# Gate and up projections as seven block products in Strassen's form, with sums of weights by adding transfers and VectorE

## The chip, the cores and the metric

The kernel runs on one core of one Trainium2 chip. A core has five engines with their own instruction streams: TensorE (PE), which multiplies matrices and loads its standing operand by separate weight loads (PEld), VectorE (DVE), ScalarE (ACT), GpSimd (POOL) and SyncE (SP), which issues transfers. [...] The metric is the device time of one execution in microseconds, the median of several runs; lower is better.

## The reference

512 tokens of width 1024 go through two layers. Each layer is half a gated FFN, a mixer (a short convolution, or attention over the tokens, each beside an attention over a memory of 256 rows), and half a gated FFN again; so there are four FFNs, each with 2816 hidden features.

```python
D_MODEL = 1024
SEQ = 512
D_FF = ((8 * D_MODEL // 3 + 255) // 256) * 256
...
def swiglu(h, w_gate_up, w_down):
    gu = h @ w_gate_up
    gate, up = gu[..., :D_FF], gu[..., D_FF:]
    return (jax.nn.silu(gate) * up) @ w_down
...
        x = x + 0.5 * swiglu(rmsnorm(x, ffn_norm[l, 0]), ffn_w_gate_up[l, 0], ffn_w_down[l, 0])
...
        x = x + 0.5 * swiglu(rmsnorm(x, ffn_norm[l, 1]), ffn_w_gate_up[l, 1], ffn_w_down[l, 1])
    return rmsnorm(x, final_norm)
```

## The kernel before

**Numbers.** Everything is held with the features on the 128 partitions and the 512 tokens along the free side, so x is eight tiles of 128x512. Values are fp32, and each operand of a product is split into two parts of type float32r, a high part (a copy that rounds) and a low part (the value less the high part). A product over 128 rows is then three matmuls, high by high, high by low and low by high (mm3, L134 to L136), each with a weight load of its own.

**Weights.** The class Weights takes the weights in pieces of 128x1024, that is 8 blocks of 128x128, in the order of use. A piece is loaded by SyncE into one of 4 buffers (wr, L63), three pieces ahead, and split two pieces ahead: the high part by ACT (wh, L81), the low part by DVE (wl, L82), into 3 buffers each. Since the buffers go round, a split waits until TensorE has read the piece that held the buffer before.

**An FFN.** Its 22 hidden tiles of 128 features stand in two halves of 11. For a hidden tile, project is called for the gate and again for up: 8 blocks of rows by mm3, 24 matmuls of 512 columns into one of 7 PSUM banks (mm). Then DVE multiplies the gate by 1 / rms of the tokens (L287), ACT takes Silu (L288), DVE multiplies by up (L289), and ACT and DVE split the hidden tile (L139, L140). The norm's gain is taken into x ahead of the products (Normed, L143), and 1 / rms behind them, so that products begin before the sums of squares (Stats, L155 and L159) are there; the matmuls that spread 1 / rms over the partitions (step1, L162 to L176, in the bank aux) stand after the first 2 of 8 blocks of the first up product. After each half, down takes 8 tiles of x, each by 11 x 3 matmuls of 512 columns; DVE adds them to x (L308, L311), and in the second half the next norm's gain and squares follow tile by tile. In the last FFN the last tile is taken by halves of 256 tokens with the final norm between (Last, L721 to L806).

**The order.** Each engine runs its instructions in the order in which the program gives them after scheduling; an instruction that waits holds what stands behind it on its engine. The core of the FFN is

```python
pg, pu = project(nd), project(nd, mid=st.step1 if begin else None)
...
nc.vector.tensor_tensor(out=t, in0=pg, in1=st.row, op=ALU.mult)
nc.scalar.activation(t, t, AF.Silu)
nc.vector.tensor_tensor(out=t, in0=pu, in1=t, op=ALU.mult)
hid.append(parts())
split(t, *hid[-1])
```

Of the kernel before, what the change touches and what calls it, by code (L numbers as in the profile page):

```python
# [16 lines left out]
P = 128  # L17
T = 512
# [4 lines left out]
HALVES = [(0, 11), (11, 22)]  # L23
# [12 lines left out]
class Weights:  # L36
    """Pieces of the weights in the order of use: loaded ahead, and split ahead into two float32r
    parts."""

    LOAD, SPLIT = 3, 2  # L40

    def __init__(self, nc, pool):
        self.nc, self.pool = nc, pool
        self.todo, self.raw, self.parts = [], {}, {}
        self.loaded = self.split = self.used = 0

    def add(self, ap, widths=(1024, 1024), step=1024):
        at = 0
        for w in widths:
            self.todo.append((ap[:, at : at + w], step))  # L50
            at += w
        assert at == ap.shape[1]

    def load(self):
        """The next piece, by transfers of step columns."""
        n = self.loaded
        self.loaded += 1
        ap, step = self.todo[n]
        w = ap.shape[1]
        self.raw[n] = self.pool.tile([P, 1024], F32, tag="wr", name=f"wr{n}", bufs=4)  # L60
        for a in range(0, w, step):
            c = slice(a, min(a + step, w))
            self.nc.sync.dma_start(out=self.raw[n][:, c], in_=ap[:, c])  # L63
            yield

    def begin(self):
        """The next piece's parts, split by step columns."""
        i = self.split
        self.split += 1
        while self.loaded < min(len(self.todo), i + 1 + self.LOAD):  # L70
            for _ in self.load():
                pass
        ap, step = self.todo[i]
        w, raw = ap.shape[1], self.raw.pop(i)
        hi = self.pool.tile([P, 1024], F32R, tag="wh", name=f"wh{i}", bufs=3)
        lo = self.pool.tile([P, 1024], F32R, tag="wl", name=f"wl{i}", bufs=3)
# [9 lines left out]

    def next(self, ahead=SPLIT):
        """The next piece's parts; the splits run ahead of it by so many pieces."""
        i = self.used
        self.used += 1  # L90
        while self.split < min(len(self.todo), i + 1 + ahead):
            for _ in self.begin():
                pass
        return self.parts.pop(i)
# [3 lines left out]
def model(ctx: ExitStack, tc: tile.TileContext, A, out):  # L98
# [13 lines left out]
    SLOTS = {"s": 66, "t": 12}  # L112
# [7 lines left out]
    def bank(tag="mm", n=T):  # L120
        bufs = {"mm": 7, "aux": 1}[tag]
        return ppool.tile([P, n], F32, tag=tag, name=name(tag), bufs=bufs)
# [5 lines left out]
    selr = cpool.tile([64, NH], F32R, name="selr")  # L128
    ident = cst[:, C_ID : C_ID + P]
    ones = cst[:, C_ONE : C_ONE + P]  # L130

    def mm3(ps, wh, wl, xh, xl, first, last):
        """One product over 128 rows: high x high, high x low, low x high."""
        nc.tensor.matmul(ps, wh, xh, start=first, stop=False)  # L134
        nc.tensor.matmul(ps, wh, xl, start=False, stop=False)  # L135
        nc.tensor.matmul(ps, wl, xh, start=False, stop=last)  # L136
# [10 lines left out]
    class Stats:  # L147
        """The squares of tiles of 128 features, summed; then 1 / rms by token."""
# [13 lines left out]
        def step1(self, c=None):  # L162
            """The sums over all features, on every partition, and their roots."""
# [14 lines left out]
        def columns(self):  # L178
            """1 / rms of the tokens of each block, by partition."""
# [10 lines left out]
    class Normed:  # L190
        """Tiles of x times a norm's gain, in two parts; 1 / rms is applied behind the product."""
# [13 lines left out]

    def plan_ffn(n):
        for a, b in HALVES:
            chunks(A["gu"][n, a:b])
            for d in range(KD):
                W.add(A["dn"][n, d][:, a * P : b * P], (6 * P, 5 * P))  # L210
# [30 lines left out]
    # The tensor engine's clock rises while it works: it does from the first transfers on.  # L241
    zero = slot(dt=F32R)
    nc.vector.memset(zero.bitcast(F32), 0.0)
    warm = bank()
    for _ in range(10):
        nc.tensor.matmul(warm, zero[:, :P], zero, start=True, stop=True)
# [4 lines left out]
    def project(nd, n=T, mid=None):  # L251
        """The next piece of weights, 128 of its columns by all rows, times tiles of tokens."""
# [8 lines left out]
    def project_tokens(nd, nb, mid={}):  # L261
        """Four pieces of weights move, 512 columns; the tokens stand: 128 of them in each bank."""
# [12 lines left out]
    def ffn(n, x, nd, st, cols, fresh=False, last=None):  # L275
        """x + swiglu / 2, and the statistics and gains of the next norms. With last, the final
        norm, which takes the last tile by halves of the tokens."""
        nst, nxt = Stats(), [Normed(c) for c in cols]
        new = list(x)
        for h, (a, b) in enumerate(HALVES):  # L280
            m = b - a
            hid = []
            for j in range(m):
                begin = st.row is None
                pg, pu = project(nd), project(nd, mid=st.step1 if begin else None)
                t = slot("t")
                nc.vector.tensor_tensor(out=t, in0=pg, in1=st.row, op=ALU.mult)  # L287
# [7 lines left out]
            for d in range(KD):  # L295
# [23 lines left out]
                if end:  # L319
                    for q in nxt:  # L320
                        q.add(d, y)
# [580 lines left out]
```

## Time and profile before

| what | value |
|---|---|
| median of 3 runs (lowest, highest) | 2036.88 us (2036.84, 2038.18) |
| span of the profiled execution | 2038.5 us |
| TensorE busy in it | 99% |
| VectorE, ScalarE, GpSimd busy | 49%, 35%, 2% |
| bytes moved | 195.73 MB |

The profile is of one execution, and its span stands beside the median as the time of that execution. Busy times are for each engine apart, in us and as a share of the span. In a timeline a row gives start and length of an instruction, its engine, line and operation, what it writes and reads, its shape, and in brackets how long the engine had stood idle and what ended that. A matmul's length holds its way through the array, which the next one overlaps, so the rate of a stream is read from the distance of the starts.

### The profile page before, as it was taken

To read this page: it belongs to the slowest core of one execution; us is meant where nothing else is said; L and a number is where in the kernel's file an instruction comes from. 1 tells how busy PE (TensorE), PEld (TensorE's weight loads), DVE (VectorE), ACT (ScalarE), POOL (GpSimd) and SP (SyncE) were. 2 spreads that over 40 slices of the span, in tenths; PEclk is the share of its full clock that TensorE was granted. 3 is DMA by queue.
4 is the path that set the end of the run, shared out by engine and by line. 5 is a ranking of instruction groups with operands and counts; after the bars stand their busy time and mean duration, and the time that the engine had idled before them with its cause. 6 is when DMAs were issued, how large, how long until landed. Compare 5 with 4: busy or idle time off the path is not lost.

```text
span 2038.5 us, 22628 instructions
## 1 busy us (share of the span) xinstructions
PE 2018.4 (99%) x9175; PEld 1674.7 (82%) x9175; DVE 1002.9 (49%) x1355; ACT 704.7 (35%) x1049; POOL 34.1 (2%) x50
## 2 busy tenths in 40 slices
PE   9999999999999999999999999999999999999997
PEld 8788888888888888888888888888878878888886
DVE  7643434576555443443644343467546664344444
ACT  7422222353224332232432222335335552222233
POOL 2000000000000000000000000000001100000000
PEclk9999999999999999999999999999999999999998
DMA  7322332332222323322322332232221032233222
GB/s 261 105 94 79 117 99 82 99 104 73 98 99 93 100 84 91 118 94 76 120 94 86 91 114 98 80 112 77 80 93 63 32 103 94 84 102 106 98 78 70
DMA packets 62328, 195.73 MB, mean 96 GB/s; under 512 B 7056, under 2 KB 9232, under 8 KB 62224
## 3 DMA queue, kind: packets, MB, share of 16 engines
q1 hardware_dynamic: 62224, 194.30, 30.0%
q8 instruction: 71, 1.16, 0.2%
q14 instruction: 33, 0.27, 0.0%
HBM read 192.17 MB, written 2.10 MB: 95 GB/s over the span
## 4 chain that ended last, share of the span: by engine, by line
PE 98%; DVE 1%; DMA 0%; issue 0%; ACT 0%; SPq 0%; DVEq 0%; ACTq 0%
PE mm L134 32%; PE mm L135 32%; PE mm L136 32%; PE mm L694 0%; PE mm L434 0%; DVE wl L82 0%; DMA s<-in_memT 0%; PE aux L651 0%; DVE s L143 0%; PE mm L666 0%; PE mm L750 0%; PE aux L134 0%; PE aux L136 0%; PE aux L135 0%; PE mm L785 0%
## 5 line engine op out<-in xcount | busy, mean ns | idle before, releaser
L134 PE MATMUL mm<-s,wh 128*128 128x512 f32 (+1 forms) x2763 | 1067.5, 386 | 2.4 <-ACT s L143 1.5
L135 PE MATMUL mm<-s,wh 128*128 128x512 f32 (+1 forms) x2763 | 1066.6, 386 | 0.3
L136 PE MATMUL mm<-s,wl 128*128 128x512 f32 (+1 forms) x2763 | 1066.0, 386 | 0.5 <-DVE wl L82 0.5
L81 ACT ACTIVATE wh<-wr 128x1024 fp32r<-128x1024 f32 (+3 forms) x403 | 390.4, 970 | 1174.1 <-PE mm L135 749.9
L134 PEld LDWEIGHTS mm<-s,wh 128*128 128x128 f32 x2763 | 519.0, 188 | 108.1 <-ACT s L143 2.4
L136 PEld LDWEIGHTS mm<-s,wl 128*128 128x128 f32 x2763 | 518.9, 188 | 105.9 <-DVE wl L82 1.1
L135 PEld LDWEIGHTS mm<-s,wh 128*128 128x128 f32 x2763 | 519.2, 188 | 104.7 <-DVE s L143 0.7
L82 DVE TENSOR_TENSOR wl<-wr,wh 128x1024 fp32r<-128x1024 f32 (+3 forms) x403 | 449.3, 1116 | 190.9 <-ACT wh L81 189.0
L289 DVE TENSOR_TENSOR t<-mm,t 128x512 f32<-128x512 f32 x88 | 60.9, 692 | 289.9 <-PE mm L136 287.0
L287 DVE TENSOR_TENSOR t<-mm,r 128x512 f32<-128x512 f32 x88 | 60.8, 691 | 224.6 <-PE mm L136 224.5
L308 DVE SCALAR_TENSOR_TENSOR t<-mm,r 128x512 f32<-128x512 f32 (+1 forms) x65 | 44.4, 683 | 124.8 <-PE mm L136 124.8
L140 DVE TENSOR_TENSOR s<-t,s 128x512 fp32r<-128x512 f32 (+1 forms) x128 | 86.4, 677 | 2.2 <-ACT s L139 2.0
L139 ACT ACTIVATE s<-t 128x512 fp32r<-128x512 f32 (+1 forms) x128 | 78.6, 616 | 16.5 <-DVE t L547 6.2
L143 DVE SCALAR_TENSOR_TENSOR s<-s,vec,s 128x512 fp32r<-128x512 f32 (+1 forms) x64 | 49.0, 780 | 14.6 <-ACT s L143 14.6
L288 ACT ACTIVATE t<-t 128x512 f32<-128x512 f32 x88 | 54.2, 616 | 3.1 <-DVE t L287 3.1
L143 ACT ACTIVATE s<-s,vec 128x512 fp32r<-128x512 f32 (+1 forms) x64 | 42.9, 688 | 33.3 <-DVE s L311 32.8
L311 DVE TENSOR_TENSOR s<-s,t 128x512 f32<-128x512 f32 (+1 forms) x65 | 45.2, 696 | 0.6
L352 DVE TENSOR_TENSOR s<-s,mm 128x512 f32<-128x512 f32 x32 | 21.8, 686 | 42.3 <-PE mm L136 42.3
L135 PE MATMUL mm<-wl,s 128*128 128x512 f32 x96 | 38.2, 398 | 4.4 <-DVE wl L82 4.4
L155 ACT ACTIVATE t<-s 128x512 f32<-128x512 f32 x59 | 35.9, 617 | 14.1 <-DVE s L311 14.1
L140 DVE TENSOR_TENSOR s<-mm,s 128x512 fp32r<-128x512 f32 (+1 forms) x56 | 34.2, 646 | 12.2 <-ACT s L139 12.1
L686 POOL TENSOR_TENSOR s<-s,s 128x128 fp32r<-128x128 f32 x32 | 13.9, 466 | 1558.8 <-ACT s L685 1558.8
(116 smaller groups left out, 743.7 us busy)
## 6 DMA issues: line engine op xcount, KB each, us to landing
wr<-in_gu SPq DMA_DIRECT2D x176, 512.0 KB, 3.7
wr<-in_dn SPq DMA_DIRECT2D x64, 384.0 KB, 3.1
wr<-in_dn SPq DMA_DIRECT2D x64, 320.0 KB, 2.9
wr<-in_ain SPq DMA_DIRECT2D x28, 512.0 KB, 3.7
wr<-in_wout SPq DMA_DIRECT2D x24, 512.0 KB, 3.7
wr<-in_mkv SPq DMA_DIRECT2D x14, 512.0 KB, 5.2
wr<-in_wq SPq DMA_DIRECT2D x8, 512.0 KB, 3.7
wr<-in_wv SPq DMA_DIRECT2D x8, 512.0 KB, 3.7
```

Source lines behind the costliest of these rows:

```text
L81: self.nc.scalar.activation(hi[:, c], raw[:, c], AF.Copy),
L82: self.nc.vector.tensor_tensor(out=lo[:, c], in0=raw[:, c], in1=hi[:, c].bitcast(F32), op=ALU.subtract),
L134: nc.tensor.matmul(ps, wh, xh, start=first, stop=False)
L135: nc.tensor.matmul(ps, wh, xl, start=False, stop=False)
L136: nc.tensor.matmul(ps, wl, xh, start=False, stop=last)
L139: nc.scalar.activation(hi, src, AF.Copy)
L140: nc.vector.tensor_tensor(out=lo, in0=src, in1=hi.bitcast(F32), op=ALU.subtract)
L143: return nc.scalar.activation(hi, src, AF.Copy, scale=g), nc.vector.scalar_tensor_tensor(out=lo, in0=src, scalar=g, in1=hi.bitcast(F32), o ...
L287: nc.vector.tensor_tensor(out=t, in0=pg, in1=st.row, op=ALU.mult)
L288: nc.scalar.activation(t, t, AF.Silu)
L289: nc.vector.tensor_tensor(out=t, in0=pu, in1=t, op=ALU.mult)
L311: nc.vector.tensor_tensor(out=y[:, c], in0=new[d][:, c], in1=t[:, c], op=ALU.add)
```

## The change

**What is computed.** Two hidden tiles make a pair. The gate and up weights of one hidden tile (an item) are a matrix of 2 x 2 blocks: gate and up by the first and the second 512 features of x. x is a matrix of 2 x 2 blocks too: first and second 512 features by first and second 256 tokens. Their product is worked out in Strassen's form (Winograd's variant), with seven block products in place of eight: each has 4 blocks of 128 rows, mm3 and 256 columns, so that a pair takes 7 x 2 x 4 x 3 = 168 matmuls of 256 columns, where it took 2 x 2 x 8 x 3 = 96 of 512. UNITS names the seven by their combination of x, in the order of use: B11, B21, T3, T4, T2, T1, B22.

**Weights.** A pair's weights are seven pieces of 128x1024: four blocks and combinations of them. Two of the sums are made by transfers: SyncE loads the first block, and a transfer issued by GpSimd adds the second to it in SBUF (tile ws, 3 buffers; lines 93 and 95). Two are made by DVE in place (L127). Each piece is split by ACT (L118) and DVE (L119) as before, seven for two hidden tiles where it was four. Buffers: wr 5, wh and wl 4, loads 8 ahead.

**x.** Quads and Quad form the seven combinations of x for the next FFN: a scaled copy by ACT, four sums of 256 columns by GpSimd for two tiles of x, and the splits of the results.

**Banks.** The 7 + 1 banks become three doubles (mm, one for an item of the pair) and two aux. Other stages take halves of the doubles.

**Behind the products**, in the class Gated: the products of the item are added up in its two banks, partly by TensorE, which adds to what stands in a bank. ACT copies B11's sum to where B21 is added (L471, the seed) and copies T3 (L475) and T2 (L477) aside; DVE adds T2 to where T4 and T3 stood (L478), adds to T1 (L480), multiplies up by -1 / rms (L482) and gate by 1 / rms (L488); ACT takes Silu (L492); GpSimd multiplies the two by halves of the tokens (L494); the split of the hidden tile is L211 and L212. TensorE starts an item's B21 behind its L471, T4 behind L475, T1 behind L478 and B22 behind L482. The next pair's first items take the double banks in turn.

**Order.** Pairs 0 to 4, down of pairs 0 to 3, pairs 5 to 7, down of 4 to 6, pairs 8 to 10, down of 7 to 10: 8, 6 and 8 hidden tiles in place of 11 and 11. Down products stay plain. step1 is called when the first pair's B11 is finished with its late rows: products of the first two rows of B11 and B21 of both items stand ahead, with a matmul of zeros that starts the third double. Between FFNs the memory's keys and values and one x are written to DRAM and read back (keep), which makes room in SBUF.

```diff
-HALVES = [(0, 11), (11, 22)]
+GROUPS = [(0, 4), (4, 7), (7, 11)]
-    LOAD, SPLIT = 3, 2
+    LOAD, SPLIT = 8, 2
+    PIECE = [0, 1, 3, 2, 0, 4, 1]
+    BUFS = {"wr": 5, "ws": 3, "wh": 4, "wl": 4}
+    def block(self, ap):
+        w = ap.shape[1] // 4
+        item = {"ap": [ap[:, i * w : (i + 1) * w] for i in range(4)], "w": w, "raw": [None] * 5}
+        self.units += [(item, q) for q in range(7)]
...
+        w, (a11, a12, a22, a21) = item["w"], item["ap"]
+        for i, first, more in {
+            0: [(0, a11, None)], 1: [(1, a12, None)], 2: [(3, a11, a21)], 3: [(4, a21, a22), (2, a22, None)]
+        }.get(q, []):
+            t = item["raw"][i] = self.tile("ws" if more is not None else "wr")
+            self.nc.sync.dma_start(out=t[:, :w], in_=first)
+            if more is not None:
+                self.nc.gpsimd.dma_start(out=t[:, :w], in_=more, accum_op=ALU.add)
...
+        for at, to, of in ((3, 0, 4), (5, 1, 0)):
+            if q == at:
+                r = item["raw"]
+                self.nc.vector.tensor_tensor(out=r[to][:, :w], in0=r[to][:, :w], in1=r[of][:, :w], op=ALU.add)
...
+    class Quad:
+        def __init__(self, b1, b2):
+            ts = slot("t"), slot("t")
+            b11, b12, b21, b22 = b1[:, :H], b1[:, H:], b2[:, :H], b2[:, H:]
+            t1, t3, t2, t4 = ts[0][:, :H], ts[0][:, H:], ts[1][:, :H], ts[1][:, H:]
+            tt = nc.gpsimd.tensor_tensor
+            tt(out=t3, in0=b22, in1=b12, op=ALU.subtract)
+            tt(out=t1, in0=b11, in1=b12, op=ALU.subtract)
+            tt(out=t2, in0=t1, in1=b22, op=ALU.add)
+            tt(out=t4, in0=t2, in1=b21, op=ALU.subtract)
+            self.of = {}
+            self.two(b11, "B11")
+            self.four(b2, "B21", "B22")
+            self.four(ts[0], "T1", "T3")
+            self.two(t2, "T2", True)
+            self.two(t4, "T4")
...
+    def order_ffn(pair, down):
+        pair(0)
+        for i, (a, b) in enumerate(GROUPS):
+            for p in range(a + 1, b):
+                pair(p)
+            if i + 1 < len(GROUPS):
+                pair(b)
+            down(i)
...
+    UNITS = ["B11", "B21", "T3", "T4", "T2", "T1", "B22"]
+    def products(items, quads, early=()):
+        nk = len(quads)
+        late = [k for k in range(nk) if k not in early]
+        qs = []
+        for it in items:
+            it.seeded = not early
+            qs.append((banks(), it.seeded))
+        held = []
+        def product(i, u, n, w, ks):
+            q, seeded = qs[i]
+            at = {"B21": 0, "T3": T + H, "T4": T + H}.get(n, T)
+            ps = q[:, at : at + H]
+            for k in ks:
+                c = slice((i * nk + k) * P, (i * nk + k + 1) * P)
+                first = k == (early or late)[0] and (n == "B11" or n == "B21" and not seeded)
+                mm3(ps, w[0][:, c], w[1][:, c], *quads[k].of[n], first, True, True, k == ks[0])
+            return ps
+        for u, n in enumerate(UNITS):
+            w = W.next()
+            for i, it in enumerate(items):
+                if u < 2 and early:
+                    ps = product(i, u, n, w, early)
+                    held.append((i, it, u, n, w))
+                else:
+                    ps = product(i, u, n, w, list(range(nk)))
+                    it(n, ps, qs[i][0])
+            if u == 1 and early:
+                third = nc.tensor.matmul(banks()[:, :H], zero[:, :P], zero[:, :H], start=True, stop=True)
+                tc.keep_in_program_order(third)
+                for i, it, u_, n_, w_ in held:
+                    it(n_, product(i, u_, n_, w_, late), qs[i][0])
...
-                pg, pu = project(nd), project(nd, mid=st.step1 if begin else None)
-                t = slot("t")
-                nc.vector.tensor_tensor(out=t, in0=pg, in1=st.row, op=ALU.mult)
-                nc.scalar.activation(t, t, AF.Silu)
-                nc.vector.tensor_tensor(out=t, in0=pu, in1=t, op=ALU.mult)
-                hid.append(parts())
-                split(t, *hid[-1])
+        class Gated:
+            def __init__(self, j):
+                self.j, self.a, self.b = j, slot("t"), slot("t")
+            def __call__(self, n, ps, q):
+                both = q.rearrange("p (a t) -> p a t", t=T)
+                y, c, z = q[:, :H], q[:, H:T], q[:, T + H :]
+                a, b = self.a, self.b
+                if n == "B11":
+                    if p_first(self.j):
+                        st.step1()
+                        turned()
+                    to = y if self.seeded else b[:, :H]
+                    nc.scalar.activation(to, ps, AF.Copy)
+                elif n == "B21" and not self.seeded:
+                    nc.vector.tensor_tensor(out=y, in0=y, in1=b[:, :H], op=ALU.add)
+                elif n == "T3":
+                    nc.scalar.activation(a[:, :H], ps, AF.Copy)
+                elif n == "T2":
+                    nc.scalar.activation(a[:, H:], ps, AF.Copy)
+                    nc.vector.tensor_tensor(out=z, in0=z, in1=a[:, H:], op=ALU.add)
+                elif n == "T1":
+                    nc.vector.tensor_tensor(out=c, in0=ps, in1=a[:, :H], op=ALU.add)
+                    nc.vector.tensor_tensor(
+                        out=b.rearrange("p (a t) -> p a t", t=H), in0=both[:, :, H:],
+                        in1=less[0].rearrange("p (a t) -> p a t", t=H), op=ALU.mult,
+                    )
+                elif n == "B22":
+                    g = slot("t")
+                    nc.vector.tensor_tensor(
+                        out=g.rearrange("p (a t) -> p a t", t=H), in0=both[:, :, :H],
+                        in1=st.row.rearrange("p (a t) -> p a t", t=H), op=ALU.mult,
+                    )
+                    nc.scalar.activation(g, g, AF.Silu)
+                    for o, i in ((slice(0, H), slice(H, T)), (slice(H, T), slice(0, H))):
+                        nc.gpsimd.tensor_tensor(out=g[:, o], in0=g[:, o], in1=b[:, i], op=ALU.mult)
+                    hid[self.j] = parts()
+                    split(g, *hid[self.j])
...
+        def pair(p):
+            products([Gated(2 * p), Gated(2 * p + 1)], quads, (0, 1) if p == 0 else ())
```

On DVE of the kernel before stand, in the second FFN, for a hidden tile and the start of the next (mm the products of gate and up, r is 1 / rms, t the tile that is worked on, s parts of hidden tiles, wr, wh and wl the pieces of the weights):

```order
L287 TENSOR_TENSOR t_467_4951<-mm_465_4895,r_461_4858 128x512
L82 TENSOR_TENSOR wl137_4923<-wr137_4805,wh137_4922 128x1024
L140 TENSOR_TENSOR s_464_4886<-t_462_4881,s_463_4885 128x512
L289 TENSOR_TENSOR t_467_4951<-mm_466_4926,t_467_4951 128x512
L82 TENSOR_TENSOR wl138_4962<-wr138_4836,wh138_4961 128x1024
L140 TENSOR_TENSOR s_469_4956<-t_467_4951,s_468_4955 128x512
L287 TENSOR_TENSOR t_472_5021<-mm_470_4965,r_461_4858 128x512
L82 TENSOR_TENSOR wl139_4993<-wr139_4889,wh139_4992 128x1024
```

Each product is read by one instruction, and a split of weights stands between two of them.

On DVE of the changed kernel stand, in the third pair of the same FFN, from the T2 products to the scaling of up (mm_547 and mm_548 are the double banks of items 0 and 1, nr is -1 / rms, ws a sum made by transfers):

```order
L119 TENSOR_TENSOR wl532_7006<-wr516_6795,wh531_7005 128x1024
L478 TENSOR_TENSOR mm_547_6843<-mm_547_6843,t_543_6839 128x256
L127 TENSOR_TENSOR wr516_6795<-wr516_6795,ws525_6913 128x1024
L119 TENSOR_TENSOR wl534_7038<-wr519_6849,wh533_7037 128x1024
L478 TENSOR_TENSOR mm_548_6844<-mm_548_6844,t_545_6841 128x256
L480 TENSOR_TENSOR mm_547_6843<-mm_547_6843,t_543_6839 128x256
L127 TENSOR_TENSOR wr519_6849<-wr519_6849,wr516_6795 128x1024
L482 TENSOR_TENSOR t_544_6840<-mm_547_6843,nr_512_6146 128x512
L480 TENSOR_TENSOR mm_548_6844<-mm_548_6844,t_545_6841 128x256
L119 TENSOR_TENSOR wl537_7092<-ws522_6882,wh536_7091 128x1024
L482 TENSOR_TENSOR t_546_6842<-mm_548_6844,nr_512_6146 128x512
```

Between the additions into the banks (L478, L480) and the scaling (L482) of the two items now stand two sums of weights (L127) and two splits (L119), and item 1's L478 stands ahead of item 0's L480.

On ACT of the changed kernel stand, from there on into the next pair (items mm_559 and mm_560):

```order
L477 ACTIVATE t_543_6839<-mm_547_6843 128x256
L118 ACTIVATE wh533_7037<-wr519_6849 128x1024
L477 ACTIVATE t_545_6841<-mm_548_6844 128x256
L118 ACTIVATE wh536_7091<-ws522_6882 128x1024
L492 ACTIVATE t_549_7055<-t_549_7055 128x512
L118 ACTIVATE wh539_7123<-wr526_6916 128x1024
L211 ACTIVATE s_550_7060<-t_549_7055 128x512
L492 ACTIVATE t_552_7076<-t_552_7076 128x512
L471 ACTIVATE mm_559_7089<-mm_559_7089 128x256
L118 ACTIVATE wh542_7154<-wr516_6795 128x1024
L211 ACTIVATE s_553_7081<-t_552_7076 128x512
L471 ACTIVATE mm_560_7090<-mm_560_7090 128x256
```

The split wh533 stands ahead of item 1's copy of T2 (L477), wh536 ahead of the Silu of item 0 (L492), and the seeds of the next pair (L471) behind Silu and split of the hidden tiles of this pair.

244 lines of the change are left out of this document (162 added, 82 removed).

## The prediction

> **What bounds the kernel now.** The page is read first: the busy shares, then the chain that ended last, then the costliest group of TensorE with the idle time ahead of it. Its columns there are busy time, mean ns of one and idle time with its releaser.
>
> ```profile
> span 2038.5 us, 22628 instructions
> PE 2018.4 (99%) x9175; PEld 1674.7 (82%) x9175; DVE 1002.9 (49%) x1355; ACT 704.7 (35%) x1049; POOL 34.1 (2%) x50
> PE 98%; DVE 1%; DMA 0%; issue 0%; ACT 0%; SPq 0%; DVEq 0%; ACTq 0%
> L134 PE MATMUL mm<-s,wh 128*128 128x512 f32 (+1 forms) x2763 | 1067.5, 386 | 2.4 <-ACT s L143 1.5
> ```
>
> TensorE holds 98% of the chain, and its commonest matmul waited 2.4 us in all. So every matmul taken away is worth its spacing, and every wait put into its stream costs its full length. The view of waits says the same: the longest one of TensorE on VectorE (total, times, longest) is
>
> ```profile
> PE mm L135 <- DVE wl L82: 4.4, 2, 3.7
> ```
>
> A stretch of the gate and up products shows the slack of the others (length, then busy time and count of PE, PEld, DVE, ACT, POOL, then granted clock, DMA share, GB/s):
>
> ```profile
> 560.00:600.00 40.00, 40.00 (x178) 33.10 (x177) 21.47 (x27) 10.65 (x12) 0.00 (x0) 1.00 0.31 105
> ```
>
> DVE is busy 54% and ACT 27% of the time there, so neither is a bound by its load; what they can cost is latency.
>
> **The price of a matmul.** The last tile of the last down product runs at 512 columns and then by halves of 256, which gives both spacings in one timeline of TensorE (start, length).
>
> ```profile
> 2004.83 0.39 PE L135 MATMUL mm<-s,wh 128*128 128x512 f32 x1
> ...
> 2015.25 0.39 PE L136 MATMUL mm<-s,wl 128*128 128x512 f32 x1
> 2015.48 0.28 PE L134 MATMUL mm<-s,wh 128*128 128x256 f32 x1
> ...
> 2018.59 0.28 PE L136 MATMUL mm<-s,wl 128*128 128x256 f32 x1
> 2018.71 0.50 PE L750 MATMUL mm<-cst,t 128*128 128x1 f32 x4
> ```
>
> From 2004.83 to 2015.48 there are 47 steps of 0.2266 us; from 2015.48 to 2018.71 there are 27 of 0.1196. I use 0.2267 and 0.120, so half the columns cost 0.53 of the time. Before: 4 FFNs x 22 tiles x 2 x 8 x 3 = 4224 gate and up matmuls, x 0.2267 = 957.6 us. After: 4 x 11 pairs x 168 = 7392 of 256 columns, x 0.120 = 887.0. **The stream gains 70.6 us**, or 21.76 - 20.16 = 1.60 a pair. The down products keep 528 matmuls in each FFN and gain nothing.
>
> The Trainium skill, "TensorE: Matmul & The Clock Gate", section Back-to-back issue gap, speaks against the change: it gives a stream of load and matmul pairs about 131 ns at 512 columns and 81 at 128, on a line between them about 98 at 256 (an estimate). By that a pair would go from 12.6 to 16.4 us and the change would lose some 170 us in TensorE alone. The trace doesn't agree: its stream of such pairs stands at 226.6 ns; the formula for an isolated matmul on the same page, 518 and 262 cycles at 2.4 GHz, lies nearer and would make the gain 104 us.
>
> **What the epilogue costs.** After an item's seven products, its two banks pass back through ACT and DVE between products, and TensorE waits for them at five places. The durations: first a gate tile of before, whose last matmul releases DVE, and ACT's split that releases DVE's.
>
> ```profile
> 99.73 0.39 PE L136 MATMUL mm<-s,wl 128*128 128x512 f32 x1
> 99.98 1.06 ACT L81 ACTIVATE wh<-wr 128x1024 fp32r<-128x1024 f32 x1 [3.83 <-PE mm L135]
> 100.16 0.69 DVE L287 TENSOR_TENSOR t<-mm,r 128x512 f32<-128x512 f32 x1 [2.70 <-PE mm L136]
> 101.08 1.23 DVE L82 TENSOR_TENSOR wl<-wr,wh 128x1024 fp32r<-128x1024 f32 x1 [0.22 <-ACT wh L81]
> ```
>
> The matmul ends at 100.12 and DVE starts at 100.16; ACT ends at 101.04 and DVE starts at 101.08: a hand-over is 0.04 us (I take 0.06 to TensorE). Queued behind one another on DVE they overlap by 0.09:
>
> ```profile
> 43.52 0.41 DVE L504 TENSOR_TENSOR t<-mm,r 128x256 f32<-128x256 f32 x1
> 43.85 1.21 DVE L82 TENSOR_TENSOR wl<-wr,wh 128x1024 fp32r<-128x1024 f32 x1
> ...
> 57.63 1.21 DVE L82 TENSOR_TENSOR wl<-wr,wh 128x1024 fp32r<-128x1024 f32 x1
> 58.76 0.74 DVE L143 SCALAR_TENSOR_TENSOR s<-s,vec,s 128x512 fp32r<-128x512 f32 x1
> ```
>
> that is 0.33 for 256 columns and 1.13 for 1024 until the next one starts, and by the same 0.09 about 0.60 for 512. The smaller forms, by group:
>
> ```profile
> L504 DVE TENSOR_TENSOR t<-mm,r 128x256 f32<-128x256 f32 x8 | 3.1, 415 | 0.0
> L139 ACT ACTIVATE s<-mm 128x256 fp32r<-128x256 f32 x8 | 3.2, 399 | 0.0
> L139 ACT ACTIVATE s<-t 128x512 fp32r<-128x512 f32 x120 | 75.5, 630 | 13.9 <-DVE t L547 6.2 <-DVE t L361 5.0 <-DVE t L289 0.8
> L479 POOL TENSOR_TENSOR t<-t 128x256 f32<-128x256 f32 x1 | 0.7, 737 | 0.1
> ```
>
> So 0.42 and 0.69 on DVE, 0.40, 0.62 and 1.06 on ACT, 0.74 for each half multiplied on POOL. One item's product is 12 x 0.12 = 1.44 us, and while TensorE is in the other item's, this item's epilogue has that long. By the order on ACT and DVE (shown above for the third pair of a later FFN):
>
> - **T1 of item 1.** The high part of a later unit's weights (L118, wh533) takes the buffer that T2 reads until its next-to-last matmul, and stands ahead of the copy and the sum (L477, L478) of item 1, with its low part. 0.04 + 1.06 + 0.04 + 1.13 + 0.42 + 0.06 = 2.75. TensorE has 2.88 - 1.48 = 1.40 left to do (T2's next-to-last matmul ends 10 x 0.12 + 0.28 into its item). Wait 1.35.
> - **B22 of item 0.** Behind that sum on DVE come the sum of T1 (L480), a sum of weights (L127) and the scaling of up (L482): 0.33 + 1.13 + 0.69 - 0.09 = 2.06 against 1.44. Wait 0.62.
> - **B22 of item 1.** The split wh536 waits in the same way for T1's buffer, and its low part stands ahead of L482 of item 1: 0.04 + 1.06 + 0.04 + 1.13 + 0.69 + 0.06 = 3.02, against 2.88 - 1.48 + 0.62 = 2.02. Wait 1.00.
> - **B21 of item 1 of the next pair** adds to a bank that L471 copies last on ACT, behind the whole way of the hidden tiles: gate scaled, Silu, two halves on POOL, split, and again from Silu for item 1: 0.69 + 0.62 + 1.48 + 0.54 + 0.62 + 1.48 + 0.54 + 0.40, with five hand-overs of 0.04 and one of 0.06, = 6.63 (0.54 being a split that the next one overlaps by 0.09). TensorE has B22 of item 1, 1.59 with the wait ahead of it, and three more items, 3 x 1.44, at hand: 5.91. Wait 0.72.
> - **T4 of item 1**: 0.07.
>
> Together 3.76 us in a full pair, 2.2 more than the 1.60 it gains: a pair goes from 21.76 to 23.92. In each FFN five pairs are full (18.8), the first costs about 3.8, two follow a down product and have no hidden tile ahead on ACT (2 x 3.1), three stand ahead of one, where the next pair's sums aren't due (3 x 2.14). That is 35.2, **x 4 = +140.8 us**.
>
> **The other terms.** The accumulating transfers are issued by POOL between two multiplications. Before, transfers are SyncE's:
>
> ```profile
> 0.74 0.40 SPq L234 DMA_DIRECT2D vec<-in_vec  x1
> wr<-in_gu SPq DMA_DIRECT2D x176, 512.0 KB, 3.7
> q1 hardware_dynamic: 62224, 194.30, 30.0%
> ```
>
> An issue of 0.40 would vanish in the 1.24 us by which POOL is idle there; if POOL were held for the 3.7 of issue to landing, 20 full pairs would wait 2.46 longer, +49. Nothing in it can gain. I take 1.6 us, four issues, nearer to the first row: **+7**. Loads go from 4 to 7 pieces a pair, from 31% to about 31 x 1.75 x 21.8 / 23.9 = 49% of the DMA engines, and run eight units ahead: nothing.
>
> Where one FFN follows another, 1 / rms is asked for after only 31 matmuls of 256 columns, 3.7 us, where it had 30 of 512, 6.8. Behind the last tile come its sum 0.69, the scaled copy 0.62, four sums on POOL 2.96, a split behind them with hand-overs 0.8, and the squares' split 0.63 + 0.69: 6.4. **+2.6, three times: 7.7.** At the start POOL has 16 sums of x and 8 of squares:
>
> ```profile
> L159 POOL TENSOR_TENSOR t<-t,t 128x512 f32<-128x512 f32 x10 | 14.9, 1494 | 39.8 <-ACT t L155 39.4
> 54.55 1.41 POOL L159 TENSOR_TENSOR t<-t,t 128x512 f32<-128x512 f32 x1 [0.27 <-ACT t L155]
> 54.76 2.28 DVE L82 TENSOR_TENSOR wl<-wr,wh 128x1024 fp32r<-128x1024 f32 x1
> ```
>
> 16 x 0.74 + 8 x 1.49 = 24 us, beside TensorE's products of the memory and ending near the first pair: from 0 to 15, I take **+4**. A split beside POOL's sum took 2.28 in place of 1.21; in a pair POOL runs while B11 and B21 do, when DVE is on no path, so this is priced at nothing, and at up to 1.7 a pair if the cover went. Six banks by halves of doubles in place of seven for the other stages: 0 to 10, **+3**.
>
> Sum: -70.6 + 140.8 + 7.7 + 4 + 7 + 3 = **+91.9**. On the execution profiled that gives 2130.4; the median of the runs lies 1.6 below its span, at 2036.88, so **2129**.
>
> **The rivals.** *The splits run early (faster).* If the high parts of wh533 and wh536 are not held by their buffers, nothing stands ahead of item 1 on ACT and DVE. Then T1 waits for copy and sum only, 0.40 + 0.42 + 0.3 = 1.1 against 1.44, B22 for 0.33 + 0.69 + 0.26 = 1.28 against 1.44: no wait. What is left is 0.72 in 20 pairs, 14.4: -70.6 + 14.4 + 21.7 = -34.5, **2002**. It decides from (70.6 - 21.7) / 44 = 1.1 us of waits a pair downward. For it: ACT and DVE are half idle. Against it: four buffers and two units of lead leave the fifth split no place but that of the product just running. Chance 0.10.
>
> *POOL is held by its transfers*: +42 on the forecast, **2171**. For it, the hidden tiles' way is the longest of the five; against it, SyncE's 0.40. Chance 0.12.
>
> *The clock drops in the waits.* It did after one wait:
>
> ```profile
> 57.10 0.50 PE L135 MATMUL mm<-wl,s 128*128 128x512 f32 x1 [3.67 <-DVE wl L82]
> 58.62 0.63 PE L134 MATMUL mm<-wh,s 128*128 128x512 f32 x1
> 59.05 0.63 PE L135 MATMUL mm<-wl,s 128*128 128x512 f32 x1
> 61.18 0.52 PE L134 MATMUL mm<-s,wh 128*128 128x512 f32 x1
> ```
>
> After 3.67 us without a matmul six stand 0.43 apart in place of 0.227, a loss of 1.2 us. My longest wait is 1.4 in a pair. If short ones added up to the same, 44 pairs would lose 1.2 to 1.5 each: +53 to 66, **about 2190**. Chance 0.06. The Trainium skill, same page, Part 1 on the clock gate, lets the clock fall after about one idle window of 3.4 us, and the trace agrees in this one wait; by that rule this rival would not come.
>
> **How the numbers follow.** Forecast 0.68, from 2085 (a wait or two of the five shorter by half, about 1 us a pair) to 2160 (the upper ends of start and banks, and half of POOL's); the faster rival 0.10, POOL 0.12, clock 0.06, and 0.04 for waits that nearly cancel the gain. The range from 2075 to 2190 leaves out the faster rival and the end of the clock's. About 0.2% is what a measurement of this kernel can tell from no change: faster 0.11, same 0.03, slower 0.86.
>
> **What would show it.** In the changed profile: spacing of 256-column matmuls 0.120 in a gate and up window; a pair's period 23.9; waits of TensorE's first matmuls of T1 and B22 on DVE (L478, L482) of 0.6 to 1.4 and of B21 on ACT (L471); ACT's L118 waiting for TensorE. A period under 21.8 would make me wrong in sign, one over 25 points to POOL, and a granted clock below 1 in those windows to the clock.

## The result and the profile after

The changed kernel takes 2312.48 us (2310.18 to 2315.22, four runs) against 2037.51 for the kernel before: a ratio of 1.135, 95% interval 1.1334 to 1.1366. It is slower by 275 us, where the forecast was 92. The page of the changed kernel, the lines that were shown of before:

```profile
span 2312.5 us, 30757 instructions
PE 2056.8 (89%) x12348; PEld 1799.3 (78%) x12348; DVE 1375.3 (59%) x1742; ACT 963.5 (42%) x1501; POOL 315.1 (14%) x378
L203 PE MATMUL mm<-s,wh 128*128 128x256 f32 (+1 forms) x3816 | 1254.6, 330 | 197.7 <-DVE t L482 38.4
```

The commonest matmul waited 2.4 us before and 197.7 now. Who is waited for, in the view of waits of TensorE (total, times, longest), its first rows:

```profile
PE mm L203 <- DVE t L482: 38.4, 64, 0.8
PE mm L203 <- ACT mm L471: 38.2, 32, 1.4
PE mm L203 <- DVE mm L478: 37.9, 32, 1.2
PE mm L203 <- DVE s L530: 22.9, 12, 3.6
PE mm L203 <- DVE s L212: 14.4, 16, 1.4
PE mm L203 <- DVE s L575: 12.8, 5, 3.6
PE mm L203 <- ACT wh L118: 12.3, 13, 2.1
PE mm L203 <- ACT t L646: 8.7, 3, 4.0
```

The first three are the waits of a pair that the prediction priced: B22 (twice), B21 and T1. The others stand outside the pairs: L530 adds a down tile, L212 is a split, here in the mixers, and L575 and L646 belong to the mixers too. For all of these stages the prediction had 3 us. Where the time lies, by stages (from TensorE's first product of gate and up and DVE's last addition of down, read from the timelines of both; ends of the last stage by the spans):

| stage | before, us | after, us | difference |
|---|---|---|---|
| until the first FFN | 61.2 | 74.6 | +13.4 |
| the four FFNs | 1452.1 | 1627.1 | +175.0 |
| mixer of layer 0 | 233.9 | 261.0 | +27.1 |
| mixer of layer 1 | 291.3 | 349.9 | +58.6 |

The mixers as windows, of before and then of after (length, busy time and count of PE, PEld, DVE, ACT, POOL, granted clock, DMA share, GB/s):

```profile
421.80:655.70 233.90, 233.90 (x1072) 194.88 (x1071) 139.13 (x191) 83.63 (x127) 0.00 (x0) 1.00 0.28 92
1373.90:1665.20 291.30, 289.89 (x1415) 239.36 (x1414) 178.26 (x332) 139.47 (x287) 13.93 (x32) 1.00 0.23 74
```

```profile
479.00:739.90 260.90, 243.98 (x1059) 197.99 (x1058) 146.63 (x198) 89.06 (x140) 15.11 (x14) 0.96 0.24 82
1547.20:1897.10 349.90, 311.01 (x1403) 246.81 (x1403) 187.97 (x341) 145.36 (x301) 32.57 (x49) 0.95 0.24 76
```

TensorE has much the same work there and was idle for 0 and 1.4 us before; now it is idle for 17 and 39 us, and runs at a lower clock for part of the rest.

A full pair came out nearly as worked out. Its four waits in TensorE's timeline, from T1 of item 1 on, and the next pair's T1:

```profile
153.05 0.39 PE L203 MATMUL mm<-s,wh 128*128 128x256 f32 x1 [1.19 <-DVE mm L478]
...
155.11 0.39 PE L203 MATMUL mm<-s,wh 128*128 128x256 f32 x1 [0.37 <-DVE t L482]
...
157.64 0.39 PE L203 MATMUL mm<-s,wh 128*128 128x256 f32 x1 [0.83 <-DVE t L482]
...
164.80 0.39 PE L203 MATMUL mm<-s,wh 128*128 128x256 f32 x1 [1.16 <-ACT mm L471]
...
177.90 0.39 PE L203 MATMUL mm<-s,wh 128*128 128x256 f32 x1 [1.18 <-DVE mm L478]
178.12 0.28 PE L206 MATMUL mm<-s,wh 128*128 128x256 f32 x1
178.24 0.28 PE L207 MATMUL mm<-s,wl 128*128 128x256 f32 x1
```

The bracket counts from the end of the matmul ahead, 0.28 after its start, so a wait beyond the spacing is the bracket plus 0.16: 1.35, 0.53, 0.99 and 1.32, where the prediction had 1.35, 0.62, 1.00 and 0.72. The next matmul then starts 0.22 later in place of 0.12, so each wait costs 0.11 more, which had no price. The pair takes 177.90 - 153.05 = 24.85 us, forecast 23.92. On DVE the row that the T1 wait hangs on stands where the order put it, behind ACT's split, which waited for TensorE (timelines of ACT and DVE):

```profile
150.34 1.06 ACT L118 ACTIVATE wh<-wr 128x1024 fp32r<-128x1024 f32 x1 [0.94 <-PE mm L206]
151.43 1.23 DVE L119 TENSOR_TENSOR wl<-wr,wh 128x1024 fp32r<-128x1024 f32 x1 [0.19 <-ACT wh L118]
152.57 0.43 DVE L478 TENSOR_TENSOR mm<-mm,t 128x256 f32<-128x256 f32 x1
```

What B21's wait has above 0.72 lies on POOL. Its adding transfer stands between the multiplications of the two items, waited for its first block and then held POOL 0.88; and the two halves of item 1 took 1.73 where those of item 0 took 1.44:

```profile
158.94 1.44 POOL L494 TENSOR_TENSOR t<-t,t 128x256 f32<-128x256 f32 x2 [9.49 <-ACT t L492]
161.47 0.88 POOL L95 DMA_DIRECT2D ws<-in_gu  x1 [1.10 <-DMA ws<-in_gu]
162.08 1.73 POOL L494 TENSOR_TENSOR t<-t,t 128x256 f32<-128x256 f32 x2
```

### The profile page after: what moved, and what is told of

Same layout as the page of the kernel before. It is cut to its first block, busy times and chain, and to the rows that moved or that the text cites. A ratio compares the mean times of both kernels' runs of the same rounds, so it can differ in the third digit from the quotient of the medians.

```text
span 2312.5 us, 30757 instructions
## 1 busy us (share of the span) xinstructions
PE 2056.8 (89%) x12348; PEld 1799.3 (78%) x12348; DVE 1375.3 (59%) x1742; ACT 963.5 (42%) x1501; POOL 315.1 (14%) x378
## 5 line engine op out<-in xcount | busy, mean ns | idle before, releaser
L203 PE MATMUL mm<-s,wh 128*128 128x256 f32 (+1 forms) x3816 | 1254.6, 330 | 197.7 <-DVE t L482 38.4
L206 PE MATMUL mm<-s,wh 128*128 128x256 f32 (+1 forms) x3816 | 1228.8, 322 | 0.6 <-DVE s L215 0.2
L207 PE MATMUL mm<-s,wl 128*128 128x256 f32 (+1 forms) x3816 | 1225.3, 321 | 0.8 <-DVE wl L119 0.8
L203 PEld LDWEIGHTS mm<-s,wh 128*128 128x128 f32 x3816 | 732.0, 192 | 308.8 <-DVE t L482 51.3
L206 PEld LDWEIGHTS mm<-s,wh 128*128 128x128 f32 x3816 | 734.6, 193 | 53.2 <-DVE s L212 4.0
L207 PEld LDWEIGHTS mm<-s,wl 128*128 128x128 f32 x3816 | 733.7, 192 | 53.7 <-DVE wl L119 1.3
L118 ACT ACTIVATE wh<-wr 128x1024 fp32r<-128x1024 f32 (+2 forms) x415 | 429.6, 1036 | 766.5 <-PE mm L206 643.9
L119 DVE TENSOR_TENSOR wl<-wr,wh 128x1024 fp32r<-128x1024 f32 (+2 forms) x415 | 524.1, 1264 | 310.9 <-ACT wh L118 310.3
L530 DVE SCALAR_TENSOR_TENSOR s<-mm,s 128x512 f32<-128x512 f32 (+1 forms) x97 | 66.4, 685 | 225.5 <-PE mm L207 225.5
L494 POOL TENSOR_TENSOR t<-t,t 128x256 f32<-128x256 f32 x176 | 140.2, 883 | 421.3 <-ACT t L492 421.3
L95 POOL DMA_DIRECT2D ws<-in_gu x88 | 77.7, 883 | 831.4 <-DMA ws<-in_gu 733.0
L118 ACT ACTIVATE wh<-ws 128x1024 fp32r<-128x1024 f32 x88 | 93.1, 1058 | 182.9 <-PE mm L206 182.9
L212 DVE TENSOR_TENSOR s<-t,s 128x512 fp32r<-128x512 f32 (+1 forms) x192 | 149.3, 785 | 31.7 <-ACT s L211 29.4
L119 DVE TENSOR_TENSOR wl<-ws,wh 128x1024 fp32r<-128x1024 f32 x88 | 107.7, 1223 | 79.9 <-ACT wh L118 79.6
L211 ACT ACTIVATE s<-t 128x512 fp32r<-128x512 f32 (+1 forms) x192 | 111.1, 583 | 81.0 <-POOL t L494 53.0
L492 ACT ACTIVATE t<-t 128x512 f32<-128x512 f32 x88 | 53.6, 622 | 79.5 <-DVE t L488 79.5
L488 DVE TENSOR_TENSOR t<-mm,r 128x512 f32<-128x512 f32 x88 | 60.4, 686 | 39.9 <-PE mm L207 39.4
L482 DVE TENSOR_TENSOR t<-mm,nr 128x512 f32<-128x512 f32 x88 | 60.3, 686 | 0.8
L212 DVE TENSOR_TENSOR s<-mm,s 128x512 fp32r<-128x512 f32 (+1 forms) x56 | 35.3, 650 | 36.0 <-ACT s L211 35.7
L127 DVE TENSOR_TENSOR wr<-wr,wr 128x1024 f32<-128x1024 f32 x44 | 54.9, 1247 | 0.4
```

What stands on the lines that cost most here:

```text
L95: self.nc.gpsimd.dma_start(out=t[:, :w], in_=more, accum_op=ALU.add)
L118: self.nc.scalar.activation(hi[:, c], raw[:, c], AF.Copy),
L119: self.nc.vector.tensor_tensor(out=lo[:, c], in0=raw[:, c], in1=hi[:, c].bitcast(F32), op=ALU.subtract),
L203: i = nc.tensor.matmul(ps, wh, xh, start=first, stop=more, skip_group_check=more)
L206: nc.tensor.matmul(ps, wh, xl, start=False, stop=more, skip_group_check=more)
L207: nc.tensor.matmul(ps, wl, xh, start=False, stop=last or more, skip_group_check=more)
```

## The experiments

Two questions: what made the time outside the pairs (theory A, the doubles; theory B, what else the change adds there), and whether the pair's waits are due to what stands ahead on ACT, DVE and POOL. All ratios are to the kernel before, measured with each.

**The doubles, alone on the kernel before.**

```diff
-        bufs = {"mm": 7, "aux": 1}[tag]
-        return ppool.tile([P, n], F32, tag=tag, name=name(tag), bufs=bufs)
+        if tag == "aux":
+            return ppool.tile([P, T], F32, tag="aux", name=name("aux"), bufs=2)
+        if not spare:
+            two = banks()
+            spare.append(two[:, T:])
+            return two[:, :T]
+        return spare.pop()
```

> The kernel before with one part of the change alone: its 7 + 1 banks become three doubles handed out by halves and two aux. Theory A (a second half of a double waits for whoever reads the first half, and a new double for both): the mixers lose about what they lose in the changed kernel, 26 + 59 us, and each up product waits some 0.8 us for the gate's reader unless other matmuls stand between: 2110 to 2200. Theory B (the mixers lose by the keys, values and x written to DRAM and read back, and by the seven splits of the next x): 2037 to 2050.

Measured 2149.57, ratio 1.055 (1.0519 to 1.0581): 112 us for this one edit, with no Strassen product in the kernel. From the last addition of down to the next FFN's first scaling of a gate its mixers take 21.5 and 47.7 us longer, and each of its eight down groups 4.2. Theory B falls. That the up products would wait for the gates' reader didn't show as such.

**Six single banks, on the kernel before.**

```diff
-        bufs = {"mm": 7, "aux": 1}[tag]
+        bufs = {"mm": 6, "aux": 2}[tag]
```

> The kernel before with 6 + 2 single banks in place of 7 + 1. If the doubles cost by their halves waiting for each other, six single banks cost little: 2037 to 2045. If it is the number of banks, most of the 112 us that the three doubles cost the kernel before: 2100 to 2150.

Measured 2038.34, ratio 1.0003 (0.9993 to 1.0014). The number of banks costs nothing; the 112 us are the form, two banks in one tile, and what the program then waits for.

**The changed kernel with single banks outside the FFNs.**

```diff
+            cm = tc.tile_pool(name=name("ppool"), bufs=1, space=PSUM)
+            psum["pool"] = cm, cm.__enter__()
...
+        if not psum["doubles"]:
+            return ppool.tile([P, T], F32, tag=tag, name=name(tag), bufs={"mm": 7, "aux": 1}[tag])
...
+        use(True)
...
+        if n != 1:
+            use(False if n < 3 else None)
```

> The changed kernel, with 7 + 1 single banks for everything outside the FFNs and the doubles inside them only. Theory A: the mixers give back most of 85 us, 2225 to 2245, and TensorE's waits in them (on ACT L646, DVE L575 and others) go. Theory B: 2300 to 2312, waits as they were.

Measured 2228.34, ratio 1.0937: 84 us less. The mixers take 234.2 and 294.1, as before the change within 3 us.

**And with single banks everywhere.**

```diff
     def banks():
-        return ppool.tile([P, 2 * T], F32, tag="mm", name=name("mm"), bufs=3)
+        return bank(), bank()
...
-            at = {"B21": 0, "T3": T + H, "T4": T + H}.get(n, T)
-            ps = q[:, at : at + H]
+            ps = q[0][:, :H] if n == "B21" else q[1][:, H:] if n in ("T3", "T4") else q[1][:, :H]
...
+                    for o, i in ((slice(0, H), c), (slice(H, T), z)):
+                        nc.vector.tensor_tensor(out=b[:, o], in0=i, in1=less[0][:, o], op=ALU.mult)
```

> The changed kernel with 7 + 1 single banks everywhere: an item takes two singles, and its two scalings (L482, L488) become two instructions of 256 columns each. Theory A: the mixers give back 85, the down products the waits of their second tile on the addition of the first (about 2 us in each of 8 down groups, up to 6 in the last ones), the pairs stay within 0.2 us of 24.9: 2190 to 2215. Theory B: 2295 to 2315.

Measured 2184.63, ratio 1.0722: 128 us less than the changed kernel. The down products show what a double does. In the changed kernel, DVE adds the first tile late, behind a split of a hidden tile, and TensorE, whose second tile lies in the other half of the same double, starts only then (timelines of DVE and TensorE):

```profile
213.21 0.69 DVE L212 TENSOR_TENSOR s<-t,s 128x512 fp32r<-128x512 f32 x1
213.82 0.68 DVE L530 SCALAR_TENSOR_TENSOR s<-mm,s 128x512 f32<-128x512 f32 x1
214.56 0.50 PE L203 MATMUL mm<-s,wh 128*128 128x512 f32 x1 [1.96 <-DVE s L530]
```

With single banks there is no such wait there. The waits of B22 are gone too, but TensorE now waits twice for the seed (L460 is L471 in the changed kernel) and, as before, for T1 (L467 is L478 there). The view of waits:

```profile
PE mm L194 <- ACT mm L460: 92.2, 64, 1.8
PE mm L194 <- DVE mm L467: 37.9, 32, 1.2
```

What B22 no longer waited, B21 did, and a pair takes 25.25 us, 0.4 more: the hidden tiles' way through POOL was behind it. This way has also become longer. In one pair POOL's two halves of item 0, beside two splits of weights on DVE, took 3.00; those of item 1, with DVE almost idle, 1.43 (timeline of POOL; L479 is L494 in the changed kernel):

```profile
149.46 3.00 POOL L479 TENSOR_TENSOR t<-t,t 128x256 f32<-128x256 f32 x2 [7.48 <-ACT t L477]
153.78 1.43 POOL L479 TENSOR_TENSOR t<-t,t 128x256 f32<-128x256 f32 x2 [1.32 <-ACT t L477]
```

**Five buffers for the parts of the weights, in the changed kernel.**

```diff
-    BUFS = {"wr": 5, "ws": 3, "wh": 4, "wl": 4}
+    BUFS = {"wr": 5, "ws": 3, "wh": 5, "wl": 5}
```

> The changed kernel with five buffers in place of four for the high and the low parts of the weights (room from 2 s and 2 t slots). My steps for T1 and B22: the splits that stand ahead of item 1 no longer wait for the product just running. T1 of item 1 then waits about 0.3 in place of 1.35, B22 about 0.65 and 0.6 in place of 0.53 and 0.99: some 1.3 us in each of 32 pairs, 2265 to 2275. Rival (the order on ACT and DVE alone makes the waits, whenever the buffers come free): 2305 to 2315.

Measured 2276.39, ratio 1.1172: 36 us less, near the figure, but not by the steps given. T1 still waits as long, B22 no more, and B21 longer:

```profile
PE mm L203 <- ACT mm L471: 51.9, 32, 1.7
PE mm L203 <- DVE mm L478: 37.9, 32, 1.2
```

So a buffer more does not take the wait from T1. Why shows with the seeds first, below.

**The seeds first.** Single banks, and the hidden tiles' Silu and what follows it queued on ACT behind the next pair's seeds:

```diff
+                    seed = nc.scalar.activation(to, ps, AF.Copy)
+                    if self.j % 2:
+                        with tc.issue_after(seed.ins):
+                            while pend:
+                                pend.pop(0)()
```

> All banks single (2184.6), and the hidden tiles' Silu, multiplications and splits are queued on ACT behind the seeds of the next pair in place of ahead of them. By my step for B21 (the seed waits because Silu, POOL and the split stand ahead of it on ACT) the two waits of B21, 1.69 and 1.65 with 0.11 each to start again, go in 32 pairs: 2065 to 2075. Rival (the time only moves to the next wait of the pair, as it did from B22 to B21 when the banks became single): 2170 to 2190.

Measured 2105.17, ratio 1.0334: 79 us less, not 115. The seed's waits went, and others came, of T4 for the copy of T3 (L468 here), which now stands behind the hidden tile's split:

```profile
PE mm L194 <- ACT t L468: 17.0, 34, 0.8
```

The same with five buffers:

> The kernel with the seeds first, and five buffers for the parts of the weights. What is left in a full pair is the wait of T1 of item 1, 1.35 and 0.11, behind a split that waits for its buffer: it should fall to 0.3 or none, 32 x 1.1 to 1.46 = 35 to 47 less than the kernel with the seeds first, 2025 to 2040. If the split costs by standing there and not by its buffer, no change from that kernel.

Measured 2081.26, ratio 1.0216: 24 less, and again T1 waits 1.18 in the bracket. With five buffers the next split is one unit further on, and it still waits for the product that is running (timeline of ACT; L470 is the copy of T2):

```profile
757.03 1.06 ACT L118 ACTIVATE wh<-ws 128x1024 fp32r<-128x1024 f32 x1 [0.94 <-PE mm L197]
757.99 0.37 ACT L470 ACTIVATE t<-mm 128x256 f32<-128x256 f32 x1
```

With four buffers and with five the splits are put as early as the buffers allow; it is the place in the queue that costs, as the run with the splits in the program's order shows below.

**GpSimd's parts, each in the changed kernel.** First the multiplication on VectorE:

```diff
-                        nc.gpsimd.tensor_tensor(out=g[:, o], in0=g[:, o], in1=b[:, i], op=ALU.mult)
+                        nc.vector.tensor_tensor(out=g[:, o], in0=g[:, o], in1=b[:, i], op=ALU.mult)
```

> The changed kernel with the multiplication of gate and up (L494) on VectorE in place of GpSimd. My chain for B21 of item 1 loses 2 x 1.48 of POOL and gains 2 x 0.8 of DVE, 1.4 us in all and POOL's transfers too, so the wait of 1.38 goes: 32 x 1.5 = 48 less, 2262 to 2270. Rival (DVE, with 59% of the span busy, is the bound in the pairs, and 2.6 us more on it in 24.9 makes other waits): 2305 to 2340.

Measured 2254.91, ratio 1.1069: 58 less. B21's waits fall from 38.2 to 11.0, and those of the down products for L530 from 22.9 to 7.4. Then the adding transfers left out:

```diff
-            if more is not None:
-                self.nc.gpsimd.dma_start(out=t[:, :w], in_=more, accum_op=ALU.add)
```

> The changed kernel without the two adding transfers of each pair, so that two of the seven pieces lack their second block. If POOL's issue and its wait for the first block's landing, between the multiplications of item 0 and 1, make what B21's wait is above my 0.72, this wait falls from 1.38 to about 0.7: 32 x 0.66 = 21 less, 2288 to 2296. If POOL is held by them elsewhere too (the start, other stages), more than 30 less. If they cost nothing on the path, 2305 to 2315.

Measured 2293.90, ratio 1.126: 18.6 less, B21's waits 23.8 in place of 38.2. The transfers' price was 18.6; I had 7. But a wait of B21 is still about 1.0 (23.8 over 28 of them, and 0.16), so about half of what it had above 0.72 stays: POOL's first half of item 1 takes 1.12 there beside the split of a hidden tile on DVE, where the other halves take 0.74.

**The splits in the program's order.** First alone, in the changed kernel:

```diff
+            h = self.nc.scalar.activation(hi[:, c], raw[:, c], AF.Copy)
+            if q is not None:
+                self.tc.keep_in_program_order(h)
...
+            if q is not None:
+                self.tc.keep_in_program_order(l)
```

> The changed kernel with one edit: the splits of a pair's weights are kept on ACT and DVE where the program writes them, behind the copies and sums of both items, in place of ahead of item 1's. My steps for T1 and B22: T1 of item 1 waits no more (1.1 against 1.44); B22 of item 0 waits about 1.0 for the sum of weights that still stands between L480 and L482, B22 of item 1 not; the seeds of B21 now stand ahead of item 1's split of the hidden tile, 5.2 against 5.8, no wait. From 4.25 and 4 x 0.11 a pair to about 1.1: 32 x 3.6 = 115 less, 2190 to 2205. Rival (the waits only move on): 2280 to 2312.

Measured 2341.43, ratio 1.149: 29 slower, where 115 faster was expected. T1's wait went as worked out. But TensorE now waits for the splits themselves (23.1 us for L120, 18.3 for L117), and in these pairs an adding transfer is issued only 7 to 9 us ahead of the sum that reads it, some 13 in the changed kernel; DVE stands still for it, 25.8 us in 18 of the 44 pairs, in front of the scaling that B22 waits for (L130 is L127 in the changed kernel, L486 is L482). That the later splits hold the buffers it needs is argued, not shown. The rows of DVE, and the wait that they make:

```profile
151.39 0.42 DVE L484 TENSOR_TENSOR mm<-mm,t 128x256 f32<-128x256 f32 x1
153.54 1.23 DVE L130 TENSOR_TENSOR wr<-wr,ws 128x1024 f32<-128x1024 f32 x1 [1.73 <-DMA ws<-in_gu]
154.68 0.68 DVE L486 TENSOR_TENSOR t<-mm,nr 128x512 f32<-128x512 f32 x1
```

```profile
PE mm L207 <- DVE t L486: 87.6, 32, 5.5
```

**The edits together**: single banks, seeds first, the hidden tiles' splits behind the copies of T3, weights' splits in order.

> Three edits together: single banks, seeds ahead of the hidden tiles' Silu with their splits behind the copies of T3, and the splits of the weights kept in the program's order. Against the kernel with the first two (2105.2) the waits of T1, 1.35, and of T4, about 0.6, with 0.11 each, should go in 32 pairs: 62 to 70 less, 2035 to 2045. Rival (the splits, now later, make TensorE wait at the next unit): 2080 to 2110.

Measured 2045.79, ratio 1.0042 (1.0025 to 1.0059). Then with the multiplication on VectorE:

> The same with the multiplication of gate and up on VectorE. If POOL no longer holds anything on the path, no change within 4 us of the kernel with the three edits. If DVE, then busy some 18 us in a pair of 20.2, falls behind, 10 to 40 slower.

Measured 2036.63, ratio 0.9994 (0.9984 to 1.0005): 9 less, which neither guess had; it equals the kernel before. What was left was 14.5 us of B22's waits behind a split and the sums of squares:

```diff
+            W.pin = not early
+            w = W.next(1 if n == "T1" else W.SPLIT)
...
+            if n == "T1":
+                W.ahead()
...
-            if q is not None:
+            if q is not None and self.pin:
```

> The kernel of the run before with two more edits: in a pair the split that stands between T1's and B22's sums on DVE is issued behind the scalings of both items, and in the first pair of an FFN the splits aren't kept in order. The wait of B22, 0.63 and 0.11, goes in some 31 pairs (23 less), and the waits of the sums of squares fall from 4.4 and 2.2 to about 2.4 and 0.9 three times (10 less): 2000 to 2010. Rival (the two splits that then stand together make TensorE wait for the next pair's weights): 2030 to 2045.

Measured 2018.76, ratio 0.9906 (0.9891 to 0.992): 18 less than the run before, about half of what was expected. Of the waits for the sums of squares, where 10 less were expected, those for their split on ACT stayed, 12.0 us in three places, and those for its low part on DVE fell from 5.0 to 1.8. And T1 waits again in the first pairs, 4.7 in four places, where the splits are no longer kept in order. Last, one row more ahead of them:

```diff
-            products([Gated(2 * p), Gated(2 * p + 1)], quads, (0, 1) if p == 0 else ())
+            products([Gated(2 * p), Gated(2 * p + 1)], quads, (0, 1, 2) if p == 0 else ())
```

> The last kernel with three of the four rows of B11 and B21, in place of two, ahead of the sums of squares in an FFN's first pair: 12 more matmuls of 256 columns, 1.4 us more cover in three places, 0 to 5 less than with two rows.

Measured 2015.98, ratio 0.9892 (0.9875 to 0.9908), the fastest of all; its difference of 2.8 from the run before lies near what the runs scatter. Its first rows of waits, where no wait of a full pair is left:

```profile
PE aux L241 <- ACT t L211: 10.9, 3, 4.9
PE mm L203 <- ACT wh L117: 10.5, 3, 6.5
PE mm L207 <- DVE wl L120: 5.0, 3, 3.8
```

## Why the prediction was right in sign and wrong in size

- **The bound** held: TensorE's stream was full, so every wait put into it cost its length.
- **The spacing** of 256 columns came out at 0.12, and so the stream's gain of about 70 us is in every run with the seven products; it shows only when the waits are gone.
- **The pair's waits** were right in their places and in their sum: 134 us against 140.8. T1 and B22 waited in 32 pairs (the first of an FFN, the five full ones and the two behind a down product), B21 in 32 (the full ones and those ahead of a down product). B21 waited about 1.35, not 0.72; the pairs ahead of a down product, priced at 2.14, waited for B21 alone. These two misses cancelled, and that they did is luck. To start again, 0.11 after each of some 128 waits, 14 us, had been left at nothing.
- **POOL beside VectorE** had been priced at nothing, since only VectorE's split was seen to lose by it. POOL loses too, and it is on B21's path: 0.3 in the pair shown of the changed kernel (1.73 against 1.44), 1.6 in that with single banks (3.00 against 1.43).
- **1 / rms** came out near its price: TensorE waited 6.9 us for the squares' split on ACT in three places, where I had 7.7 (by the prediction's own terms, 6.4 less 3.7, it would have been 8.1).
- **The step that failed is the banks**: "Six banks by halves of doubles in place of seven for the other stages: 0 to 10, +3". They cost 128 us in the changed kernel: 84 outside the FFNs, the rest within them and at the start. I priced a count of banks, and the count is free. What costs is that the half of a double waits for the reader of the other half, in the down products too, for which the prediction had "gain nothing" and no loss. The rows of a down product show it; in the mixers it could also be that a new double waits for both halves of an old one, which was not taken apart. These 128 are most of the 183 us by which the forecast was short.
- **The adding transfers** were under-sized: 18.6 where I took 7, inside the bounds of 0 and 49.
- **The start** came to 13.4 where I took 4, inside 0 to 15. With single banks everywhere the first FFN begins 10 us earlier, so most of this belongs to the banks as well.
- **The clock** fell after more waits than I gave it: 63 us of matmuls at half pace against 3 before, a loss of some 31 (counted by the distance of the starts, 0.43 for 512 columns and 0.21 for 256, without the kernel's first microseconds). Nearly all of it lies outside the full pairs. With single banks everywhere 25 us of such matmuls are left, so more than half of this loss stands in the banks' 128 already.
- **The faster rival** named what has to go, but not the means: not buffers but the order on ACT and DVE, and the banks with it. With both mended the time goes below that of before, to 2016, though not to its 2002.

The 55 us beside the banks are these other terms, above all starting again, the adding transfers and what is left of the clock; they were not divided further by runs.

## What to carry to other kernels

When a change turns one-bank tiles into tiles of two, price what waits for the other half in every stage that borrows them, not the number of banks. A wait that is taken away often only uncovers the next one in the same queue, so work out the second before counting on the first; here only several edits together gave the gain. And more buffers do not move an instruction out of the way when the scheduler fills them at once: set its place in the queue.

## What the runs showed of the hardware that was not expected

The clock fell after waits far shorter than the 3.67 us quoted in the prediction. In the second FFN's first down group, after 1.96 us without a matmul, TensorE's timeline reads:

```profile
875.43 0.50 PE L203 MATMUL mm<-s,wh 128*128 128x512 f32 x1 [1.96 <-DVE s L530]
...
876.37 0.63 PE L203 MATMUL mm<-s,wh 128*128 128x512 f32 x1
876.80 0.63 PE L206 MATMUL mm<-s,wh 128*128 128x512 f32 x1
...
878.93 0.63 PE L203 MATMUL mm<-s,wh 128*128 128x512 f32 x1
879.36 0.45 PE L206 MATMUL mm<-s,wh 128*128 128x512 f32 x1
```

Seven matmuls stand 0.43 apart. The same wait of 1.96 us stands in the first down group of all four FFNs; such a stretch followed it in the second and the fourth, and not in the first and the third, so the length of a wait alone does not decide. The waits of up to 1.4 us in the full pairs were not followed by one. The Trainium skill, "TensorE: Matmul & The Clock Gate", Part 1 on the clock gate, has the clock fall after an idle window of about 3.4 us; this trace does not agree that a wait must be so long.
